# A hybrid decoder layer: the second products' sums and low parts on GpSimd, and more pairs by quarters

## The chip, the cores and the metric

The kernel runs on one core of one Trainium2 chip. A core has five engines that work at the same time and are ordered only by semaphores: TensorE (PE, matmuls and transposes; a weight load, PEld, overlaps the matmul), VectorE (DVE), ScalarE (ACT), GpSimd (POOL), and SyncE (SP), which issues the loads. Each engine takes its own instructions strictly in order. SBUF is the working memory, 128 partitions wide; PSUM holds the matmuls' results. The metric is the device time of one execution in microseconds (us).

## The reference, cut to what matters

One decoder layer on 512 tokens of width 1024, in float32: a gated feed-forward block (SwiGLU, inner width 2816), a mixer of two recurrences, and a second feed-forward block, each inside two RMS norms with a residual.

```python
def swiglu_ffn(x, w_in, w_out):
    gate, up = jnp.split(x @ w_in, 2, axis=-1)
    return (jax.nn.silu(gate) * up) @ w_out

x = x + 0.5 * rms_norm(swiglu_ffn(rms_norm(x, norm_pre[l, 0]), ffn1_w_in[l], ffn1_w_out[l]), norm_post[l, 0])
mixed = token_mixer(rms_norm(x, norm_pre[l, 1]), w_mix_in[l], conv_w[l], ...)
x = x + rms_norm(mixed, norm_post[l, 1])
x = x + 0.5 * rms_norm(swiglu_ffn(rms_norm(x, norm_pre[l, 2]), ffn2_w_in[l], ffn2_w_out[l]), norm_post[l, 2])
```

The change concerns the second product of both feed-forward blocks, the gated values (512 x 2816) times `w_out` (2816 x 1024).

## The kernel before, in words

**Three matmuls for one.** Every float32 operand is split into a high part (a rounded copy, made by ScalarE) and a low part (operand minus high part, made by a subtraction on VectorE). A product is then high x high, high x low and low x high (`mm3` and its like).

**First product (`ffn_in`, `prod`, line 572).** The inner width is 11 pairs of 256 columns (`PAIRS`). Each pair is made by the seven products of a Strassen-like scheme on quarters of the operands; sums of raw weights are made on the spot (line 263; the early ones on GpSimd, the later on VectorE). `ORDER` is the order of the products, written out by hand. The gated values land in `hf`.

**Second product (`ffn_out`).** The 1024 output columns are made in two halves of 512. In each half the 11 pairs of inner rows are gone through in the order `OUT[half]`; in the second half the last four (`LAST`: pairs 1, 3, 5, 7) are done token block by token block at the end, since norms and transposes hang on them. A pair is done in one of two ways:

- plain (`plain`, line 854): 4 token blocks x 2 column groups x 2 inner blocks x 3 = 48 matmuls of 256 columns;
- by quarters (`quartered`, `product`, line 862), for the pairs listed in `QUARTERED[half]`: seven products of 6 matmuls, 42 in all. Some go straight into the sums `C`, four into shared sums `M`, which `common` and `add` (line 824) bring into `C` once per half.

**What a pair needs.** A plain pair needs the high and low part of its gated values (`h_tile`, 1024 columns in one piece) and one split of its weights. A quartered pair needs three quarters of its gated values split (`h_quarters`: a subtraction of 256 and one of 512 columns), four sums of quarters (`h_sums`, line 805, four instructions of 256 columns), the split of these sums (`s_tile`, 1024 columns), and two splits of its weights: three quarters of them (768 columns), then four sums on the raw tile (`sum_quarters`, line 280) and a split of these (1024 columns). All copies are ScalarE's (lines 247 and 773), all subtractions and sums VectorE's (lines 249, 280, 774, 805). A pair that is quartered in both halves keeps its quarters and sums (`kept`; the sums then lie in `hf` itself, `stay`), otherwise the sums pass through the one buffer `hsum`. Pairs in `AGAIN` are plain in both halves and keep their split from the first.

**What sets the order.** `more(n)` writes the preparation of pairs two to three ahead of their use, and a scheduler orders each engine's instructions in advance; the first sums of early pairs thus stand among the first product's work. Buffers bound how far ahead anything runs: three tiles `s` for the splits of sums or plain pairs (`s_place`), places in the transposed input `xq` (`PLACES`, `LATER`) or in the ring of raw weights (`once`) for quarters, and four tiles for split weights (`WBUF`), which `feed` keeps full. Loads go out on SP's queue when a planner finds their buffer free (`load_due`). VectorE's queue also holds the work on PSUM between the products (line 591).

Of the kernel before, what the change touches and what calls it, by code (L numbers as in the profile page):

```python
# [8 lines left out]
F32 = mybir.dt.float32  # L9
F32R = mybir.dt.float32r  # L10
AF = mybir.ActivationFunctionType
ALU = mybir.AluOpType
# [41 lines left out]

QUARTERED = [(2, 3, 4, 6, 7, 8), (2, 4, 6, 8)]
OUT = [list(range(PAIRS)), [9, 2, 4, 10, 6, 8, 0, 1, 3, 5, 7]]
LAST = 4
PLACES, LATER = {2: 1, 4: 2, 6: 0, 8: 3}, {0: (1, 0), 7: (2, 3)}  # L60

AGAIN, ROWS = (9, 10), (18, 19, 20, 21)

# [24 lines left out]
class Layer:  # L90
# [678 lines left out]
            out.append(t[:, o : min(o + D, 2 * D)])  # L769
        return out  # L770

    def two_parts(self, hi, lo, src):
        self.nc.scalar.copy(hi, src)  # L773
        self.nc.vector.tensor_tensor(lo, src, hi.bitcast(F32), op=ALU.subtract)

    def h_tile(self, k2, dst=None):

        hi, lo = dst or self.s_place()
        src = self.hf[:, 2 * k2 : 2 * k2 + 2, :]
        self.two_parts(hi, lo, src)  # L780
        return hi, lo

    def h_quarters(self, k2, n=None):
# [14 lines left out]
    def h_sums(self, k2, stay):  # L798

        a = self.by_chunk(k2)  # L800
        f = self.hf[:, 2 * k2 : 2 * k2 + 2, :]
        if not stay:
            f = self.sp.tile([P, 2, T], F32, tag="xn", bufs=1, name=self.nm("hsum"))
        v = f.rearrange("p k (c u t) -> p k u c t", u=2, t=P)
        tt = lambda out, x, y, op: self.nc.vector.tensor_tensor(out, x, y, op=op)
        tt(v[:, 0, 0], a[:, 0, 1], a[:, 0, 0], ALU.subtract)
        tt(v[:, 1, 0], v[:, 0, 0], a[:, 1, 0], ALU.add)
        for k in range(2):
            tt(v[:, k, 1], a[:, k, 1], v[:, 1, 0], ALU.subtract)
        return f  # L810
# [8 lines left out]
    def ffn_out(self, gpost_row, scale, after, trans, head):  # L819
# [3 lines left out]
        nc, mm = self.nc, self.nc.tensor.matmul  # L823
        tt = lambda out, a, b, op: nc.vector.tensor_tensor(out, a, b, op=op)
        seq = [(half, k2) for half in range(2) for k2 in OUT[half]]
        made = deque((h, None) for h in self.hs)
# [3 lines left out]
        def more(n):  # L830
            while count[0] < min(n, len(seq)):
                half, k2 = seq[count[0]]
                count[0] += 1
                if k2 in QUARTERED[half]:
                    if k2 not in kept:
                        stay = k2 in QUARTERED[1]
                        kept[k2] = self.h_quarters(k2, PLACES.get(k2)), self.h_sums(k2, stay)
                    a, f = kept[k2]
                    made.append((a, self.s_tile(f)))
                elif half and k2 in AGAIN:  # L840
                    made.append(again.popleft())
                else:
                    made.append((self.h_tile(k2, self.x_place(*LATER[k2]) if half and k2 in LATER else None), None))
                    if not half and k2 in AGAIN:
                        again.append(made[-1])

# [56 lines left out]
        for half in range(2):  # L903
            C = [[self.ps() for _ in range(2)] for _ in range(2)]
            M, T, left = None, None, len(QUARTERED[half])
            for m, k2 in enumerate(OUT[half][: PAIRS - LAST * half]):
                more(n + 2)
                h, sums = made.popleft()
                if sums:
                    begin = M is None  # L910
                    if begin:
                        M = {p: self.ps() for p in ("p1", "p5", "p7", "p6")}
                    quartered(C, M, h, sums, begin)
                    left -= 1
                    if left == 0:
                        T = common(M, [self.hf[:, j, :] for j in ROWS] if half else [self.st("c") for _ in range(4)])
                else:
                    w = self.pull()
                    more(len(seq) if half and m == PAIRS - LAST - 1 else n + 3)
                    for i in (0, 2, 1, 3):  # L920
                        for v in range(2):
                            plain(C, w, h, i, v, m == 0)
                        if i > 1 and T and m == PAIRS - 1:
                            add(C, T, i % 2)
                    self.drop(w)
                n += 1
                if n == 1:
                    self.prod("p4", PAIRS - 1)
                    self.after("p4", PAIRS - 1)
                self.lag()  # L930
# [4 lines left out]
        for k2 in OUT[1][-LAST:]:  # L935
            ws.append(self.pull())
            more(n + 1)
            n += 1
# [95 lines left out]
    def ffn_items(self, name, w_in, w_out):  # L1034
# [31 lines left out]
        for h in range(2):  # L1066
            for k2 in OUT[h]:
                src = w_out[k2 * 2 * P : (k2 + 1) * 2 * P, h * 512 : (h + 1) * 512].rearrange("(k p) d -> p k d", p=P)
                key = (name, "out", h, k2)
                made.append(Item(key, [Load(key, src, 2, 512, "raw2", 5, 8)], sums=k2 in QUARTERED[h]))  # L1070
                if k2 in QUARTERED[h]:
                    made.append(Item(key, ()))
# [682 lines left out]
```

## Time and profile before

| | |
|---|---|
| median of 3 runs | 941.69 us (941.43 to 942.03) |
| profiled execution: device time, span | 942.79 us, 941.0 us |
| TensorE busy, granted clock (mean) | 932.7 us (99%), 0.998 |
| VectorE, ScalarE, GpSimd busy | 765.2, 507.7, 116.8 us |
| second products, plain and quartered pairs | from 225.4 to 342 us, and from 819.0 to 935 us |

How to read the rows: a group has its line, engine and operation, then output <- inputs by the program's names with their size, the count, the busy time in us and the mean ns of one, and last the idle time before them with what ended it. `ps` is PSUM, every other name SBUF. A timeline row has start, duration, engine, line, operation and count; a bracket gives the idle time before it and its releaser. A row of waits tells who waited for whom: total us, times, longest. A row of windows has the stretch, its length, the busy time (and count) of TensorE, its weight loads, VectorE, ScalarE and GpSimd, then the granted clock of TensorE, the share of the DMA engines and GB/s. In the slices a digit is the busy share of a fortieth of the span in tenths.

### The profile page before, as it was taken

The page shows a single profiled execution, that of the slowest core. Times are in us where ns is not written, and L with a number is a line of the kernel's source. Part 1 is how long each engine was busy: PE and PEld are TensorE (multiplying, and loading weights), DVE is VectorE, ACT ScalarE, POOL GpSimd, SP SyncE. Part 2 cuts the span into 40 slices and gives each one's busy share as a digit, 9 for nine tenths or more (in the row PEclk, how much of TensorE's full clock was granted, in tenths as well). Part 3 has the DMA queues.
Part 4 walks back from the last instruction along what each step waited for, and adds up shares of the span by engine and source line. Part 5 has one row for each costly group of instructions (what it writes and reads, how often), then busy time and mean ns, then how long its engine had stood idle before and what let it go on. Part 6 is the DMA issues. An engine that isn't in the chain of part 4 may idle for free.

```text
span 941.0 us, 18079 instructions
## 1 busy us (share of the span) xinstructions
PE 932.7 (99%) x7495; PEld 898.7 (96%) x7495; DVE 765.2 (81%) x1036; ACT 507.7 (54%) x729; POOL 116.8 (12%) x176
## 2 busy tenths in 40 slices
PE   9999999999999999999999999999999999999997
PEld 7999999999999999998887888899999999999997
DVE  6799988889988876698846665698998888998884
ACT  7645555557456467956632444565455455755541
POOL 2530000000001045200001310354000000000101
PEclk9999999999999999999999999999999999999999
DMA  9243343332352024321312124323433432224212
GB/s 314 90 156 92 121 127 113 92 111 73 116 172 90 24 86 125 107 68 46 90 45 68 46 88 135 105 77 110 138 96 108 128 120 90 91 86 127 82 46 90
DMA packets 81676, 96.12 MB, mean 102 GB/s; under 512 B 4117, under 2 KB 61497, under 8 KB 81594
## 3 DMA queue, kind: packets, MB, share of 16 engines
q1 hardware_dynamic: 81306, 94.44, 32.7%
q8 instruction: 59, 0.97, 0.4%
q10 hardware_dynamic: 288, 0.52, 0.2%
q14 instruction: 23, 0.19, 0.1%
HBM read 92.85 MB, written 2.10 MB: 101 GB/s over the span
## 4 chain that ended last, share of the span: by engine, by line
PE 62%; ACT 0%; DVE 0%; issue 0%; POOL 0%; DVEq 0%; POOLq 0%; ACTq 0%
PE ps L572 23%; PE ps L854 7%; PE ps L504 6%; PE ps L862 5%; PE ps L153 5%; PE ps L155 5%; PE ps L154 5%; PE ps L1245 2%; PE ps L321 1%; PE ps L514 1%; PE ps L1419 0%; PE ps L1330 0%; PE ps L1499 0%; PE ps L1526 0%; PE ps L1285 0%; PE ps L1523 0%
## 5 line engine op out<-in xcount | busy, mean ns | idle before, releaser
L247 ACT CAST w<-raw 128x1024 fp32r<-128x1024 f32 (+1 forms) x234 | 240.4, 1033 | 234.6 <-PE ps L572 84.4
L249 DVE TENSOR_TENSOR w<-raw,w 128x1024 fp32r<-128x1024 f32 (+1 forms) x234 | 289.4, 1243 | 41.7 <-ACT w L247 41.1
L572 PE MATMUL ps<-xq,w 128*128 128x256 f32 x2016 | 237.7, 277 | 0.2 <-ACT hf L599 0.2
L572 PEld LDWEIGHTS ps<-xq,w 128*128 128x128 f32 x2016 | 233.4, 188 | 0.4 <-ACT hf L599 0.4
L572 PE MATMUL ps<-sq,w 128*128 128x256 f32 x1440 | 169.7, 276 | 0.0
L572 PEld LDWEIGHTS ps<-sq,w 128*128 128x128 f32 x1440 | 166.5, 188 | 0.0
L854 PE MATMUL ps<-w,hs 128*128 128x256 f32 x960 | 113.0, 276 | 0.0
L854 PEld LDWEIGHTS ps<-w,hs 128*128 128x128 f32 x960 | 110.7, 188 | 0.0
L263 DVE TENSOR_TENSOR raw<-raw,raw 128x1024 f32<-128x1024 f32 x64 | 78.3, 1224 | 1.9
L153 PE MATMUL ps<-w,xq 128*128 128x512 f32 x192 | 78.9, 411 | 0.1
L155 PE MATMUL ps<-w,xq 128*128 128x512 f32 x192 | 74.9, 392 | 0.0
L154 PE MATMUL ps<-w,xq 128*128 128x512 f32 x192 | 74.8, 391 | 0.0
L409 POOL TENSOR_SCALAR col<-col 128x1 f32<-128x1 f32 x24 | 7.9, 328 | 516.4 <-ACT junk L408 516.3
L862 PE MATMUL ps<-w,hs 128*128 128x256 f32 x480 | 57.7, 276 | 0.0
L504 PE MATMUL ps<-xq,w 128*128 128x256 f32 x480 | 56.4, 278 | 0.0
L862 PEld LDWEIGHTS ps<-w,hs 128*128 128x128 f32 x480 | 55.9, 188 | 0.0
L504 PEld LDWEIGHTS ps<-xq,w 128*128 128x128 f32 x480 | 55.2, 188 | 0.5 <-issue 0.5
L263 POOL TENSOR_TENSOR raw<-raw,raw 128x1024 f32<-128x1024 f32 x16 | 42.1, 2639 | 29.5 <-DVE w L249 28.0
L153 PEld LDWEIGHTS ps<-w,xq 128*128 128x128 f32 x192 | 36.1, 188 | 8.2 <-issue 0.9
L155 PEld LDWEIGHTS ps<-w,xq 128*128 128x128 f32 x192 | 36.0, 188 | 8.2 <-DVE xq L328 0.3
L773 ACT CAST hs<-hf 128x1024 fp32r<-128x1024 f32 x32 | 33.6, 1051 | 17.7 <-PE ps L862 10.8
L154 PEld LDWEIGHTS ps<-w,xq 128*128 128x128 f32 x192 | 36.2, 188 | 6.7 <-issue 0.2
(257 smaller groups left out, 1177.7 us busy)
## 6 DMA issues: line engine op xcount, KB each, us to landing
raw<-in_ffn_w_in_dram SPq DMA_DIRECT2D x88, 512.0 KB, 4.0
raw<-in_ffn_w_out_dram SPq DMA_DIRECT2D x44, 512.0 KB, 3.8
raw<-in_w_mix_in_dram SPq DMA_DIRECT2D x28, 512.0 KB, 3.7
raw<-in_w_mix_out_dram SPq DMA_DIRECT2D x8, 512.0 KB, 3.9
out_dram<-xs SPq DMA_DIRECT2D x8, 256.0 KB, 2.0
xs<-in_x_dram SPq DMA_DIRECT2D x6, 256.0 KB, 4.4
gpost<-in_norm_post_dram SPq DMA_DIRECT2D x3, 512.0 KB, 3.5
gpre<-in_norm_pre_dram SPq DMA_DIRECT2D x2, 512.0 KB, 4.3
```

What stands on the lines that cost most here:

```text
L153: mm(ps, sh, mh, start=start, stop=False, **kw)
L154: mm(ps, sh, ml, start=False, stop=False, **kw)
L155: mm(ps, sl, mh, start=False, stop=stop, **kw)
L247: nc.scalar.copy(hi, raw)
L249: self.low = nc.vector.tensor_tensor(lo, raw, hi.bitcast(F32), op=ALU.subtract)
L263: (nc.vector if late else nc.gpsimd).tensor_tensor(o, o, c, op=ALU.add)
L504: mm(ps[:, u0:u1], w[:, a, k, :], self.xop(k, b, u0, u1), start=k + n + m == 0, stop=k == ND - 1 and n == 2, skip_group_check=True,)
L572: self.nc.tensor.matmul(ps[:, c], wb[b][:, k, v], left[d][:, k, :], start=first and a + n + k == 0, stop=n == 2 and k == KH - 1, skip_grou ...
L773: self.nc.scalar.copy(hi, src)
L854: mm(out, a[kk][:, i * P : (i + 1) * P], w[:, b, kk, QUARTER * v : QUARTER * (v + 1)], start=begin and c == kk == n == 0, stop=kk == 1 and ...
L862: mm(ps[:, QUARTER * c : QUARTER * (c + 1)], A[a][:, c], B[b], start=begin and c == n == 0, stop=n == 2, skip_group_check=True,)
L1245: nc.tensor.matmul(sc[:, 64 * m : 64 * m + 64], k8[:, m], q8[:, m], start=True, stop=True)
```

## The change

- The four sums in `h_sums` are made by GpSimd instead of VectorE.
- `two_parts` makes the low part on GpSimd unless told otherwise; `h_quarters` and `s_tile` use that. `h_tile` stays on VectorE in the first half and goes to GpSimd in the second.
- `QUARTERED` grows: in the first half pairs 2 to 9 are quartered (5 and 9 are new), in the second 2, 4, 0, 6 and 8 (0 is new). Pair 9 leaves `AGAIN`, so its plain split is made anew for the second half. Pairs 5 and 9, and 0 in the second half, have no place in `PLACES`; their quarters go to the ring of raw weights.

ScalarE's copies, the split of all weights and the sums of raw weights (lines 247, 249, 280) stay where they are. The change adds two lines: what is line 773, 774, 805, 824, 854 and 862 before is 774, 775, 806, 825, 856 and 864 after; lines up to 572 keep their numbers.

```diff
-QUARTERED = [(2, 3, 4, 6, 7, 8), (2, 4, 6, 8)]
+QUARTERED = [(2, 3, 4, 5, 6, 7, 8, 9), (2, 4, 0, 6, 8)]
 OUT = [list(range(PAIRS)), [9, 2, 4, 10, 6, 8, 0, 1, 3, 5, 7]]
...
-AGAIN, ROWS = (9, 10), (18, 19, 20, 21)
+AGAIN, ROWS = (10,), (18, 19, 20, 21)
...
-    def two_parts(self, hi, lo, src):
+    def two_parts(self, hi, lo, src, engine=None):
+
         self.nc.scalar.copy(hi, src)
-        self.nc.vector.tensor_tensor(lo, src, hi.bitcast(F32), op=ALU.subtract)
-
-    def h_tile(self, k2, dst=None):
+        (engine or self.nc.gpsimd).tensor_tensor(lo, src, hi.bitcast(F32), op=ALU.subtract)
+
+    def h_tile(self, k2, dst=None, engine=None):
 
         hi, lo = dst or self.s_place()
         src = self.hf[:, 2 * k2 : 2 * k2 + 2, :]
-        self.two_parts(hi, lo, src)
+        self.two_parts(hi, lo, src, engine or self.nc.vector)
         return hi, lo
...
-        tt = lambda out, x, y, op: self.nc.vector.tensor_tensor(out, x, y, op=op)
+        tt = lambda out, x, y, op: self.nc.gpsimd.tensor_tensor(out, x, y, op=op)
         tt(v[:, 0, 0], a[:, 0, 1], a[:, 0, 0], ALU.subtract)
         tt(v[:, 1, 0], v[:, 0, 0], a[:, 1, 0], ALU.add)
         for k in range(2):
...
-                    made.append((self.h_tile(k2, self.x_place(*LATER[k2]) if half and k2 in LATER else None), None))
+                    dst = self.x_place(*LATER[k2]) if half and k2 in LATER else None
+                    made.append((self.h_tile(k2, dst, nc.gpsimd if half else None), None))
```

## The prediction

> **What bounds the kernel now.** First the page: busy shares and the slices of the span.
>
> ```profile
> PE 932.7 (99%) x7495; PEld 898.7 (96%) x7495; DVE 765.2 (81%) x1036; ACT 507.7 (54%) x729; POOL 116.8 (12%) x176
> PE   9999999999999999999999999999999999999997
> DVE  6799988889988876698846665698998888998884
> POOL 2530000000001045200001310354000000000101
> ```
>
> TensorE has no hole but at the very end, VectorE is second, GpSimd almost empty. The waits of TensorE, asked next, are two, together 1.7 us:
>
> ```profile
> PE ps L149 <- POOL ident masks.py:199: 1.5, 1, 1.5
> PE ps L572 <- ACT hf L599: 0.2, 1, 0.2
> ```
>
> So the time is the number of matmuls times their rate, as long as every operand is ready. The timeline of TensorE in the second products (both feed-forward blocks) gives the rate and the deadlines; the first row below is VectorE's, the start of the preparation (first quarters of the gated values):
>
> ```profile
> 210.62 1.02 DVE L774 TENSOR_TENSOR xq<-hf,xq 128x256 fp32r<-128x256 f32 x2
> 225.44 5.60 PE L854 MATMUL ps<-w,hs 128*128 128x256 f32 x48
> 230.88 2.88 PE L572 MATMUL ps<-xq,w 128*128 128x256 f32 x24
> 239.03 1.52 PE L862 MATMUL ps<-w,xq 128*128 128x256 f32 x12
> 240.40 2.88 PE L862 MATMUL ps<-w,hs 128*128 128x256 f32 x24
> 243.12 0.84 PE L862 MATMUL ps<-w,xq 128*128 128x256 f32 x6
> 243.79 1.52 PE L862 MATMUL ps<-w,once 128*128 128x256 f32 x12
> 273.04 16.48 PE L854 MATMUL ps<-w,hs 128*128 128x256 f32 x144
> 832.63 1.52 PE L862 MATMUL ps<-w,xq 128*128 128x256 f32 x12
> 866.63 16.48 PE L854 MATMUL ps<-w,hs 128*128 128x256 f32 x144
> ```
>
> A plain pair takes 48 matmuls, 230.88 - 225.44 = 5.44 us; a pair by quarters 42, 243.79 - 239.03 = 4.76 us. Pair 2 starts at 239.03, and pair 9 of the first half, still plain, runs from 273.04 to 278.48. The second block has the same distance: 866.63 - 832.63 = 34.00, as 273.04 - 239.03. I work out one block and double it.
>
> **The change, part 1: matmuls.** Pairs 5 and 9 in the first half and 0 in the second become quartered, in both blocks: 6 x (5.44 - 4.76) = -4.1 us if nothing waits.
>
> **Part 2: what VectorE gets and loses.** Prices, from the groups by form, GpSimd's line 263, and the timelines:
>
> ```profile
> L263 POOL TENSOR_TENSOR raw<-raw,raw x16: 2392/2410/3437, 23.9 to 648.4; 128x1024 f32<-128x1024 f32 x16
> L774 DVE TENSOR_TENSOR hs<-hf,hs 128x1024 fp32r<-128x1024 f32 x32 | 39.0, 1219 | 1.3 <-ACT hs L773 1.2
> L805 DVE TENSOR_TENSOR hf<-hf 128x256 f32<-128x256 f32 x32 | 13.3, 421 | 0.6
> 247.25 2.42 DVE L249 TENSOR_TENSOR w<-raw,w 128x1024 fp32r<-128x1024 f32 x2
> 250.72 0.95 DVE L249 TENSOR_TENSOR w<-raw,w 128x768 fp32r<-128x768 f32 x1
> 257.50 1.81 DVE L280 TENSOR_TENSOR raw<-raw 128x256 f32<-128x256 f32 x4
> 259.40 1.05 ACT L247 CAST w<-raw 128x1024 fp32r<-128x1024 f32 x1 [3.32 <-DVE raw L280]
> 283.45 0.19 POOL L409 TENSOR_SCALAR col<-col 128x1 f32<-128x1 f32 x1 [225.49 <-ACT junk L408]
> ```
>
> The weights of a quartered pair cost VectorE a low part of 768 columns, four sums and a low part of 1024: 0.95 + 1.81 + 1.21 = 3.97 us, where a plain one costs 1.21. What leaves VectorE per freshly quartered pair is four sums (4 x 0.42), two quarter subtractions (256 and 512 columns, 1.02 together by the 210.62 row) and one of 1024 (1.22), some 3.9 us.
>
> **Part 3: the same work on GpSimd.** The trace has only the 1024-column form there: 2.41 us alone. An instruction on one column takes 0.19, so a straight line through both gives 0.77 for 256 columns and 1.31 for 512 (estimates). In the built order GpSimd does eight sums during the first products, well ahead. From the first quarters on it has, until pair 9 can start, 33 instructions of 256 columns, 8 of 512 and 8 of 1024 (eight pairs' quarters and low parts, 25 sums). Alone that is 25.4 + 10.5 + 19.3 = 55.2 us: started at 210.62 it ends at 265.8, ahead of pair 9 at 239.03 + 7 x 4.76 = 272.4. Were this all, nothing would wait.
>
> **Part 4: the two engines exclude each other.** Timeline rows of the places where GpSimd already runs such an addition:
>
> ```profile
> 23.93 4.89 POOL L263 TENSOR_TENSOR raw<-raw,raw 128x1024 f32<-128x1024 f32 x2 [2.66 <-DVE w L249]
> 25.99 0.69 DVE L354 TENSOR_TENSOR xq<-ps,xq 128x512 fp32r<-128x512 f32 x1 [0.94 <-ACT xq L355]
> 27.91 1.99 DVE L249 TENSOR_TENSOR w<-raw,w 128x1024 fp32r<-128x1024 f32 x1 [0.25 <-ACT w L247]
> 41.51 2.39 POOL L263 TENSOR_TENSOR raw<-raw,raw 128x1024 f32<-128x1024 f32 x1 [6.65 <-DVE w L249]
> 42.40 2.59 DVE L249 TENSOR_TENSOR w<-raw,w 128x1024 fp32r<-128x1024 f32 x1 [0.36 <-ACT w L247]
> 52.13 1.22 DVE L249 TENSOR_TENSOR w<-raw,w 128x1024 fp32r<-128x1024 f32 x1
> 52.17 5.80 POOL L263 TENSOR_TENSOR raw<-raw,raw 128x1024 f32<-128x1024 f32 x2 [1.17 <-DVE col L1092]
> 53.27 2.35 DVE L1093 TENSOR_TENSOR col<-prm,col 128x4 f32<-128x4 f32 x1
> 56.22 2.83 DVE L249 TENSOR_TENSOR w<-raw,w 128x1024 fp32r<-128x1024 f32 x1
> 636.69 2.35 DVE L249 TENSOR_TENSOR w<-raw,w 128x1024 fp32r<-128x1024 f32 x2
> 637.98 5.67 POOL L263 TENSOR_TENSOR raw<-raw,raw 128x1024 f32<-128x1024 f32 x2 [7.03 <-DVE w L249]
> ```
>
> GpSimd runs from 41.51 to 43.90; a weight subtraction put out at 42.40 ends at 44.99, 1.09 after it, so it stood still meanwhile. The same at 27.91 (ends 1.08 after 28.82) and 56.22 (1.08 after 57.97). Even four columns at 53.27 took 2.35 us. It holds the other way: at 637.98 the pair ends at 643.65, 4.61 after VectorE's 639.04, so the first of the two took 4.61 - 2.41 = 2.20 from there. A subtraction that reads PSUM (25.99, 0.69 us) isn't held. So a GpSimd addition and a VectorE instruction with both inputs in SBUF take turns, instruction by instruction, and their times add. The Trainium skill says the same ("SBUF — State Buffer", section "Who interferes with whom"): a VectorE instruction with two SBUF inputs and a GpSimd one that reads SBUF contend, and the second blocks until the first is done. The trace agrees (2.59 against 1.21 us); by that rule the change loses, and without it the time would be part 1's.
>
> Everything VectorE does for weights (lines 249, 280) is of that kind, so the sum of both queues is what counts. A GpSimd instruction that waited for its turn has its start-up behind it: 2.22 for 1024 columns (2.41 - 0.19), and by the same cut 1.12 and 0.58. I take these, since 49 of them meet about as many of VectorE's; the prices alone (55.2) are the upper end. GpSimd: 33 x 0.58 + 8 x 1.12 + 8 x 2.22 = 45.9 us. VectorE in the same stretch: six of 1024 columns (the last first-product weights, pairs 0, 1 and 10) 7.3, and eight pairs' weights 8 x 3.97 = 31.8, together 39.0. So the last weights of pair 9 are ready at 210.62 + 45.9 + 39.0 = 295.5; the 24 matmuls on them take 2.72 (240.40 to 243.12), and pair 9 ends at 298.2 instead of 278.5: +19.7. With the prices alone it is +29.0. The faster matmuls of pairs 5 and 9 are lost in this wait.
>
> To that come stretches in which neither can go. Between a pair's sums and its last low part ScalarE copies the weights (1.05, the 259.40 row) and VectorE waits; GpSimd fills this except where its own next instruction waits for a later ScalarE copy, by the built order at pairs 7, 8 and 9: 3 x 1.05 = 3.2. Bounds: 0, and all eight, 8.4.
>
> **Part 5: the second half.** Per quartered pair both queues need 2.22 + 3.97 = 6.2 against 4.76: 7.2 us too much over five, and pair 0's quarters and sums 3.4 more. The plain pairs 10, 9 and again 10 give back 2 x 4.2 + 2.0 = 10.4. Nothing left, so 0; bounds -1 and +5. Pair 0 saves 0.68. The low part of pair 5, the third of the last four, can start when pair 0's sums leave their buffer (0.68 before pair 0 ends) and is wanted 2.72 after: 3.4 us for 1.05 + 2.41 and a VectorE turn of 1.21, so +1.3. Pair 9 is no longer kept, which is one 1024 more, counted above. Pairs 5, 9 and 0 put their quarters into the ring of raw weights, so two loads for the mixer, and what stands behind them on SP's queue, go out at pair 0's end; four plain pairs (4 x 5.44 = 21.8 us) hide them; without these a landing of some 4 us would show.
>
> **Sum.** Per block 19.7 + 3.2 + 0 - 0.7 + 1.3 = 23.5 us, twice 47.0. The profiled execution took 942.79 us (span 941.0) and gives 989.8; the median of 941.69 gives **989 us**, 5% slower.
>
> **Rivals.** (a) The turns don't bind here and GpSimd alone matters: its queue is done at 265.8, pair 9 wants it at 272.4, TensorE never waits, 941.69 - 4.1 = **937.6 us**, faster. For it: 6.6 us of slack, and VectorE is relieved of 6 x 3.9 + 9 x 1.22 - 3 x 2.76 = 26 us per block (nine 1024-column low parts of the second half leave it too; three pairs' weights are added). Against: every GpSimd addition that met a weight subtraction held it. It decides from the point where both queues together fit between 210.62 and 272.4 (61.7 us); I count 84.9.
>
> (b) The stalls also lower TensorE's clock. The windows at the end of the span show that it falls:
>
> ```profile
> 935.00:938.00 3.00, 0.00 (x0) 0.00 (x0) 1.84 (x3) 0.45 (x2) 0.81 (x2) 0.99 0.00 0
> 938.00:941.00 3.00, 0.00 (x0) 0.00 (x0) 0.00 (x0) 0.00 (x0) 0.00 (x0) 0.50 0.47 175
> ```
>
> The third number from the right is the granted clock: 0.99, then 0.50, once TensorE has had no matmul for about 3 us (its last here end at 934.8). The Trainium skill states it as a rule ("TensorE: Matmul & The Clock Gate", section "What's actually happening"): after an idle window of about 3.4 us the clock is halved until one such window has been busy; the trace agrees at this one place. My sum leaves 298.2 - 239.0 - 8 x 4.76 = 21 us of holes in eight pairs, under 3 us each, so I take the full clock. At half clock a pair takes 9.52 and the eight end at 239.0 + 76.2 = 315.2, 17 us later; if that holds for half of the stretch, twice 8.5 is added: **1006 us**.
>
> (c) The change could fail to do what it says, if the built program kept the sums on VectorE or the pairs plain. It doesn't: the built order shows them on GpSimd and 42 matmuls for each new pair. No chance is set aside.
>
> **How the numbers follow.** The taking of turns has every meeting in the trace behind it, so the forecast of 989 us gets 0.73; its own range is 981 (no idle stretches, -1 in the second half: 2 x 4.2 less) to 1028 (per block +9.3 for the prices alone, +5.2 for all idle stretches, +5 in the second half). Rival (a) has 0.10, since the short forms and saturated queues appear nowhere; rival (b) 0.15; a stall that just eats the 4 us 0.02. The range of 968 to 1030 leaves out (a); it takes in (b) and 13 us below the forecast's own low end, as the 84.9 us of both queues rest on two estimated forms (33 x 0.58 + 8 x 1.12 = 28.1; a quarter less is 7 per block). Faster by over 0.2% 0.10, within 0.2% (2 us, about what runs of this kernel, 941.43 to 942.03, can tell from no change) 0.02, slower 0.88.
>
> **What would show it.** Part 1: 36 matmuls fewer. Part 3: GpSimd's busy time up by some 2 x 80 us or more, since waiting counts as busy there. Part 4: VectorE's line 249 mean well above 1243 ns, GpSimd's 256-column form far above 0.77 where both are busy; TensorE idle behind line 249's low parts or line 775's in pairs 3 to 9 of the first half, in both blocks; pair 9 ending about 20 us later. Part 5: few holes in the second half. Rival (a) shows a TensorE without holes; (b) a granted clock below 1.00 in the first half. I would be wrong if turns go by something other than whole instructions, if the short forms cost much more than the line through two points, or if the in-order queues lock each other out for longer than I counted.

## The result and the profile after

The changed kernel takes 1016.57 us (median of 4 runs, 1015.07 to 1018.4) beside 941.86 us for the kernel before on the same chip: 1.0791 times the time before, 95% interval 1.0769 to 1.0813. Its profiled execution has a span of 1015.0 us, 74.0 more than before, and a mean granted clock of 0.979 instead of 0.998.

The page of the changed kernel, busy shares, the slices of TensorE and of its clock:

```profile
PE 956.2 (94%) x7459; PEld 913.6 (90%) x7459; DVE 818.4 (81%) x960; ACT 516.3 (51%) x749; POOL 342.3 (34%) x320
PE   9999999998688799999999999999999999778877
PEclk9999999999899899999999999999999999989989
```

There are 36 matmuls fewer, as forecast, and still TensorE is busy for 23.5 us longer. The holes lie in two stretches, the second products of the two blocks. The waits of TensorE in the changed kernel (for whom, us in total, times, longest):

```profile
PE ps L864 <- ACT w L247: 29.6, 16, 4.9
PE ps L864 <- DVE w L249: 14.4, 18, 0.9
PE ps L864 <- DVE y L446: 3.9, 2, 2.0
PE ps L864 <- POOL hs L775: 1.9, 2, 0.9
PE ps L149 <- POOL ident masks.py:199: 1.5, 1, 1.5
PE ps L856 <- POOL hs L775: 0.8, 2, 0.5
```

That is 52.1 us of waits where the kernel before had 1.7. The additional 50.4 us of waits and 23.5 us of busy time make up the 74.0 us. Of the waits 44.0 us are for weights (lines 247 and 249), 3.9 for the norm between the halves (`y`) and only 2.7 for a low part that GpSimd makes. So TensorE hardly waits for GpSimd itself; it waits for the engines that make the weights. VectorE's and GpSimd's groups by form show the cause:

```profile
L249 DVE TENSOR_TENSOR w<-raw,w 128x1024 fp32r<-128x1024 f32 x214 | 290.2, 1361 | 62.8 <-ACT w L247 62.0
L280 DVE TENSOR_TENSOR raw<-raw 128x256 f32<-128x256 f32 x104 | 103.9, 999 | 3.2
L249 DVE TENSOR_TENSOR w<-raw,w 128x768 fp32r<-128x768 f32 x26 | 43.7, 1681 | 3.3 <-ACT w L247 3.3
L775 POOL TENSOR_TENSOR hs<-hf,hs 128x1024 fp32r<-128x1024 f32 x26 | 70.0, 2697 | 62.6 <-ACT hs L774 62.6
```

A sum of raw weights (line 280) takes 999 ns on the mean, 0.42 us in the kernel before; the low part of 768 columns 1681 ns, 0.95 before; a low part of 1024 columns on GpSimd takes 2.70 us, where 2.41 is what one takes alone. Both engines stand still in turn, and standing still counts as busy.

Where the time goes within a block is read from TensorE's timeline. First half of the columns, first block:

```profile
237.85 1.52 PE L864 MATMUL ps<-w,xq 128*128 128x256 f32 x12
...
256.12 0.58 PE L864 MATMUL ps<-w,hs 128*128 128x256 f32 x1 [3.19 <-ACT w L247]
257.44 3.99 PE L864 MATMUL ps<-w,hs 128*128 128x256 f32 x17 [0.73 <-DVE w L249]
...
266.93 2.27 PE L864 MATMUL ps<-w,hs 128*128 128x256 f32 x17 [0.88 <-DVE w L249]
...
274.10 0.38 PE L864 MATMUL ps<-w,hs 128*128 128x256 f32 x1 [2.08 <-ACT w L247]
275.36 3.42 PE L864 MATMUL ps<-w,hs 128*128 128x256 f32 x17 [0.88 <-DVE w L249]
...
296.47 1.60 PE L864 MATMUL ps<-w,once 128*128 128x256 f32 x12
...
301.30 11.04 PE L856 MATMUL ps<-w,hs 128*128 128x256 f32 x96
```

Pair 2 starts at 237.85 and pair 9 ends at 301.30: 63.45 us, where the kernel before needed 278.48 - 239.03 = 39.45. The first half lost 24.0 us. The rows at 256.12 and 257.44 also show the clock: after a hole of 3.19 us, seventeen matmuls take 3.99 us, which take 2.27 us at 266.93. A shorter hole, 2.08 us with one matmul and 0.88 us more behind it, was enough to slow part of the next seventeen (3.42 us at 275.36). Pair 9 itself, from 296.47 on, runs through without a wait; the time is lost in the pairs before it. Second half of the columns:

```profile
314.28 1.64 PE L864 MATMUL ps<-w,xq 128*128 128x256 f32 x12 [1.94 <-DVE y L446]
...
348.84 0.58 PE L864 MATMUL ps<-w,hs 128*128 128x256 f32 x1 [4.82 <-ACT w L247]
350.10 4.00 PE L864 MATMUL ps<-w,hs 128*128 128x256 f32 x17 [0.68 <-DVE w L249]
...
354.93 3.11 PE L856 MATMUL ps<-w,hs 128*128 128x256 f32 x26
...
379.55 5.66 PE L514 MATMUL ps<-xq,w 128*128 128x256 f32 x44
```

Line 514, the work behind the second products, starts at 379.55; before it started at 343.17. From the end of pair 9 that is 78.25 us against 64.69: the second half lost another 13.6 us. Pair 0 alone, from 341.42 to 354.93, takes 13.5 us, of which 4.82 are one wait and then the half clock. What VectorE, ScalarE and GpSimd do around that wait:

```profile
338.40 5.56 POOL L775 TENSOR_TENSOR hs<-hf,hs 128x1024 fp32r<-128x1024 f32 x2 [4.85 <-ACT hs L774]
341.74 5.90 DVE L280 TENSOR_TENSOR raw<-raw 128x256 f32<-128x256 f32 x4
343.91 2.52 POOL L775 TENSOR_TENSOR xq<-hf,xq 128x1024 fp32r<-128x1024 f32 x1
347.75 1.99 ACT L247 CAST w<-raw 128x1024 fp32r<-128x1024 f32 x2 [7.74 <-DVE raw L280]
```

The four sums of pair 0's weights (1.81 us when nothing holds them) come out at 341.74, while GpSimd is in the second of three low parts of 1024 columns. They end at 347.64, after the third (346.43). ScalarE has waited 7.74 us for them, TensorE 4.82. The windows of the changed kernel give the clock by stage (columns as in the profile before):

```profile
238.00:301.00 63.00, 47.35 (x335) 44.67 (x334) 54.00 (x46) 25.39 (x33) 45.28 (x31) 0.89 0.23 69
301.00:355.00 54.00, 44.80 (x360) 43.32 (x359) 46.86 (x51) 24.50 (x39) 28.90 (x21) 0.94 0.25 77
885.00:940.00 55.00, 42.74 (x302) 40.87 (x303) 47.90 (x45) 22.29 (x28) 36.91 (x26) 0.88 0.25 77
```

### The profile page after: what moved, and what is told of

Same layout as the page of the kernel before. It is cut to its first block, busy times and chain, and to the rows that moved or that the text cites. A ratio compares the mean times of both kernels' runs of the same rounds, so it can differ in the third digit from the quotient of the medians.

```text
span 1015.0 us, 18156 instructions
## 1 busy us (share of the span) xinstructions
PE 956.2 (94%) x7459; PEld 913.6 (90%) x7459; DVE 818.4 (81%) x960; ACT 516.3 (51%) x749; POOL 342.3 (34%) x320
## 5 line engine op out<-in xcount | busy, mean ns | idle before, releaser
L247 ACT CAST w<-raw 128x1024 fp32r<-128x1024 f32 (+1 forms) x240 | 244.3, 1027 | 305.9 <-DVE raw L280 128.8
L249 DVE TENSOR_TENSOR w<-raw,w 128x1024 fp32r<-128x1024 f32 (+1 forms) x240 | 333.0, 1395 | 66.1 <-ACT w L247 65.2
L864 PE MATMUL ps<-w,hs 128*128 128x256 f32 x624 | 96.7, 308 | 45.9 <-ACT w L247 29.6
L864 PEld LDWEIGHTS ps<-w,hs 128*128 128x128 f32 x624 | 86.1, 211 | 53.4 <-ACT w L247 32.8
L806 POOL TENSOR_TENSOR hf<-hf 128x256 f32<-128x256 f32 x40 | 43.6, 1099 | 227.4 <-DVE hf L591 226.1
L280 DVE TENSOR_TENSOR raw<-raw 128x256 f32<-128x256 f32 x104 | 103.9, 999 | 3.2
L856 PE MATMUL ps<-w,hs 128*128 128x256 f32 x768 | 91.6, 277 | 0.8 <-POOL hs L775 0.8
L775 POOL TENSOR_TENSOR hs<-hf,hs 128x1024 fp32r<-128x1024 f32 x26 | 70.0, 2697 | 62.6 <-ACT hs L774 62.6
L856 PEld LDWEIGHTS ps<-w,hs 128*128 128x128 f32 x768 | 89.1, 188 | 1.2 <-POOL hs L775 1.2
L864 PE MATMUL ps<-w,xq 128*128 128x256 f32 x288 | 41.1, 294 | 3.9 <-DVE y L446 3.9
L153 PEld LDWEIGHTS ps<-w,xq 128*128 128x128 f32 x192 | 36.1, 188 | 8.2 <-issue 0.9
```

Source lines behind the costliest of these rows:

```text
L153: mm(ps, sh, mh, start=start, stop=False, **kw)
L247: nc.scalar.copy(hi, raw)
L249: self.low = nc.vector.tensor_tensor(lo, raw, hi.bitcast(F32), op=ALU.subtract)
L280: self.nc.vector.tensor_tensor(b[out], b[a], b[c], op=ALU.add)
L775: (engine or self.nc.gpsimd).tensor_tensor(lo, src, hi.bitcast(F32), op=ALU.subtract)
L856: mm(out, a[kk][:, i * P : (i + 1) * P], w[:, b, kk, QUARTER * v : QUARTER * (v + 1)], start=begin and c == kk == n == 0, stop=kk == 1 and ...
```

## The experiments

The theory on test is Part 4's: GpSimd's additions and VectorE's two-input instructions exclude each other, and that makes the weights late. Its rivals: that the additional quartered pairs alone cost the time, that it is waits of GpSimd's own chain, and, later, whether the sum of both engines' times or the order of their work sets the loss.

**The engines alone, the pairs alone.** The first kernel keeps the new engines with the old pairs, the second the new pairs with all work on VectorE.

```diff
# engines alone (against the changed kernel)
-QUARTERED = [(2, 3, 4, 5, 6, 7, 8, 9), (2, 4, 0, 6, 8)]
+QUARTERED = [(2, 3, 4, 6, 7, 8), (2, 4, 6, 8)]
-AGAIN, ROWS = (10,), (18, 19, 20, 21)
+AGAIN, ROWS = (9, 10), (18, 19, 20, 21)
# pairs alone: the same two lines the other way, against the kernel before
```

> The change of engines without the new quartered pairs (six in the first half, four in the second, as before). Turns (VectorE and GpSimd exclude each other where both read SBUF): a quartered pair takes about 8.4 us in the first half instead of 4.76, as in the changed kernel, six of them, less the slack of the plain pair 5: about 15 us per block there and 5 in the second half, so 982 us (965 to 1000). Rival, GpSimd is simply too slow for eight pairs: with six its queue ends earlier still, 942 us. Rival, the weights of the added pairs are the cost: 942 us.

Measured: 970.04 us, ratio 1.0297 (1.0280 to 1.0314), so 28 us slower: within the range, 12 under the figure.

> The new quartered pairs without the change of engines: all sums and low parts on VectorE. Turns: GpSimd is idle, so only VectorE's own queue counts; up to pair 9 it holds 39.0 us for weights and 28.5 for the moved work, 67.5 from 210.6, so pair 9 ends near 281 instead of 278.5: 2 to 6 us more per block, 946 us (938 to 956). Rival, the added pairs are the cost of the change: about 1016 us.

Measured: 949.53 us, ratio 1.0076 (1.0061 to 1.0091), 7.5 us slower. This is within the range. The pairs save 36 matmuls (4.1 us) and lose more than that: behind the start-up TensorE waits 4.6 us, 3.7 of them for the weights of quartered pairs, and part of the remainder is a slower rate of the matmuls, told at the end of this section. The two parts cost 28 and 7.5 us alone and 74.7 together, so they are not independent. My reading is that the new pairs give VectorE more sums and low parts of weights exactly where GpSimd's additions hold it.

**Additional work on GpSimd, nothing else changed.** Two pairs of kernels add work to GpSimd in the kernel before, at the places where the change gives it work; VectorE keeps all of its own. In the first pair GpSimd reads the tiles of the second products:

```diff
+    def extra(self, x, like):       # after each low part and sum of VectorE's
+        ...
# extra reads
+        self.nc.gpsimd.tensor_tensor(o, x, x, op=ALU.subtract)
# extra writes: one column read, then two fills
+        self.nc.gpsimd.tensor_copy(one(o), one(x))
+        for _ in range(2):
+            self.nc.gpsimd.memset(o, 0.0)
```

> The kernel before, all work where it was, and beside it about the same additions once more on GpSimd (both inputs from the same SBUF tiles, result into a scratch tile that nobody reads; 1024 columns as two of 448, 512 as 448). Nothing in the products waits for a GpSimd result. Turns: VectorE is held anyway, and it still has its own 7.9 us per quartered pair, so slower than the change of engines alone, 1010 us (985 to 1045), and the mean of the weight subtractions (line 249) goes up by 10% or more. Rival, the change loses because TensorE waits for GpSimd's results: 942 us.

Measured: 1006.67 us, ratio 1.0688 (1.0661 to 1.0716), with VectorE's sums of raw weights at 711 ns instead of 422. The time is as forecast; the mean of the weight subtractions (line 249) rose by 4% (1298 ns instead of 1243), not by 10% or more.

> The same extra work on GpSimd, but as memsets of the scratch tile: each a copy of one column, for the place in time, and two memsets of 256 or 448 columns, so GpSimd is busy about as long and reads next to nothing. Turns only where GpSimd reads SBUF (so the Trainium skill, SBUF - State Buffer, Who interferes with whom): 942 us (940 to 948). Rival, any GpSimd instruction holds VectorE: near the time with extra reads, 985 us or more.

Measured: 982.92 us, ratio 1.0437 (1.0414 to 1.0461): a miss by 41 us. VectorE was not held (its sums take 421 ns, its weights 1269). What the forecast overlooked: the one-column copies read the tiles of the ring, so that a buffer comes free only when GpSimd's queue has passed it. ScalarE's timeline in the run with fills:

```profile
260.87 1.04 ACT L774 CAST hs<-hsum 128x1024 fp32r<-128x1024 f32 x1 [8.40 <-POOL scratch L792]
```

TensorE's largest wait there, 14.2 us in two, is another one: for `y` of line 446, which comes up again with the next two kernels. The run with reads has no such wait of ScalarE for GpSimd; ScalarE waits there for VectorE's sums of raw weights, 103.7 us in all against 33.5 in the kernel before. So the two runs lose their time in different ways and can't be set against each other. The second pair of kernels starts GpSimd's work from a tile of its own that ScalarE fills (at the places of the sums from one column of the gated values). The additions read `xs`, the tile of the residual stream, which the second products leave alone until their post norm; it is not the table of constants that the forecast below names. Up to the end of pair 9 no engine waits for a result of this work.

```diff
# both; 204 additions, at the low parts and sums of the kernel before
+            mark = self.hp.tile([P, 1], F32, tag="mark", bufs=16, name=self.nm("mark"))
+            self.nc.scalar.copy(mark, hi[...])
+        self.nc.gpsimd.tensor_copy(o[:, :1], mark)
# reads
+        self.nc.gpsimd.tensor_tensor(o, self.xs[:, 0, :n], self.xs[:, 1, :n], op=ALU.subtract)
# fills
+        for _ in range(2):
+            self.nc.gpsimd.memset(o, 0.0)
```

> The kernel before, unchanged in what VectorE and TensorE do; beside it GpSimd makes 204 additional subtractions of two operands, 128x192 each, into a scratch tile, at the places where the changed kernel gives it low parts and sums; they read a table of constants and not the tiles of the second products, so that no buffer of the ring waits for GpSimd's queue (ScalarE copies one column into a small tile of its own, and GpSimd starts from that). If an addition with two operands keeps VectorE out while it runs: some 150 us of additions, about half of them in the bound stretches: 980 us (962 to 1000), with the mean of the 128x1024 weights over 1290 ns against 1270. If the loss of the changed kernel came only from longer waits of its own chains: 942 to 947 us, and unchanged VectorE means.

> The same with the addition replaced by two fills (no operand read) of the same scratch tile: the same queue and the same starts, but nothing that reads with two operands. If only GpSimd's work with two operands keeps VectorE out: 943 us (940 to 950). If any use of GpSimd at these places costs, or the one-column copies do: about as much as the run with additions.

Measured: 1023.33 us with reads (1.0853, 1.0837 to 1.0869), 978.48 us with fills (1.0376, 1.0357 to 1.0395). Both lie above what I wrote, the fills by 35 us. TensorE's waits, of the run with fills and then of the run with reads, name the reason:

```profile
PE ps L882 <- DVE y L446: 25.7, 2, 12.8
```
```profile
PE ps L881 <- DVE y L446: 37.7, 4, 18.0
PE ps L881 <- ACT w L247: 5.2, 2, 2.7
PE ps L881 <- DVE w L249: 4.1, 6, 1.2
```

`y` of line 446 belongs to the post norm between the halves, and its column steps (line 409) run on GpSimd too. In the run with fills they stood behind the additional work until 302.45, and ScalarE waited 16.9 us for them. That part is the price of GpSimd's queue, which I forgot for this place. The first half of the columns lies ahead of it and is free of it. With fills TensorE starts pair 2 at 237.62 and the plain pairs at 271.62, 34.00 us apart as in the kernel before; with reads 280.86 - 238.74 = 42.12 us. VectorE's groups, of the run with fills and then of the run with reads:

```profile
L280 DVE TENSOR_TENSOR raw<-raw 128x256 f32<-128x256 f32 x80 | 33.7, 421 | 1.6
L249 DVE TENSOR_TENSOR w<-raw,w 128x768 fp32r<-128x768 f32 x20 | 19.0, 949 | 0.0
```
```profile
L280 DVE TENSOR_TENSOR raw<-raw 128x256 f32<-128x256 f32 x80 | 47.5, 594 | 1.7
L249 DVE TENSOR_TENSOR w<-raw,w 128x768 fp32r<-128x768 f32 x20 | 22.4, 1118 | 0.0
```

So GpSimd instructions with two operands in SBUF, on data that the second products don't touch there, hold VectorE and cost 8.1 us per block in that stretch; fills of the same tile at the same places hold nothing and cost it nothing. The Trainium skill ("SBUF — State Buffer", section "Who interferes with whom") says that a GpSimd instruction that only writes doesn't contend with a VectorE instruction of two SBUF inputs; the means of 421 and 949 ns agree.

**The second half given back to VectorE.**

```diff
# against the changed kernel
-                    made.append((a, self.s_tile(f)))
+                    made.append((a, self.s_tile(f, nc.vector if half else None)))
...
-                    made.append((self.h_tile(k2, dst, nc.gpsimd if half else None), None))
+                    made.append((self.h_tile(k2, dst, nc.vector if half else None), None))
```

> The changed kernel with the low parts of the second half of the columns given back to VectorE (pair 0's sums stay with GpSimd, the first half is as in the changed kernel). My account after the result: the second half lost 13.6 us per block because VectorE's chains stood behind GpSimd's 128x1024 low parts one after another; without them most of it comes back: 995 us (985 to 1003), pair 0's wait for ScalarE's weights under 1 us instead of 4.8. If the second half's loss is only what the first half's delay leaves behind, or pair 0's quarters themselves: 1010 to 1017 us.

Measured: 996.72 us, ratio 1.0572 (1.0555 to 1.0589). The wait of pair 0 is gone, and 19.9 us of the 27 us that the second halves had lost come back. Pair 0's quarters stay with GpSimd in this kernel, like its sums. The first half is as slow as in the changed kernel: from pair 2 at 238.43 to the end of pair 9 at 302.90, 64.47 us.

**Which of the two kinds of work.** One kernel gives VectorE back the sums, one the low parts.

```diff
# sums back
-        tt = lambda out, x, y, op: self.nc.gpsimd.tensor_tensor(out, x, y, op=op)
+        tt = lambda out, x, y, op: self.nc.vector.tensor_tensor(out, x, y, op=op)
# low parts back
-        (engine or self.nc.gpsimd).tensor_tensor(lo, src, hi.bitcast(F32), op=ALU.subtract)
+        (engine or self.nc.vector).tensor_tensor(lo, src, hi.bitcast(F32), op=ALU.subtract)
-                    made.append((self.h_tile(k2, dst, nc.gpsimd if half else None), None))
+                    made.append((self.h_tile(k2, dst, nc.vector if half else None), None))
```

> The changed kernel with the 80 sums of 128x256 given back to VectorE (0.42 us each there, about 0.80 on GpSimd when nothing holds it); the low parts stay with GpSimd. If the two engines take turns, the stretches that they bound get shorter by about 80 x (0.80 - 0.42) = 30 us: 986 us (968 to 1000). If GpSimd's queue for itself were the limit: 80 x 1.1 = 88 us off it, and the kernel falls to 940 to 955. If VectorE's own work were the limit: 34 us more, 1035 to 1050.

Measured: 1016.32 us, ratio 1.0785 (1.0767 to 1.0803), no gain at all. All three figures missed. The total hides two effects that cancel. Ahead of the second products one of VectorE's sums now stands behind a low part of GpSimd's (1.51 us instead of 0.42) and holds up VectorE's work on PSUM, so that TensorE waits in the first product:

```profile
215.84 2.98 PE L572 MATMUL ps<-sq,w 128*128 128x256 f32 x24 [1.37 <-DVE ps L591]
```

Pair 2 starts at 240.42 instead of 237.85. Pair 9 ends at 301.05 instead of 301.30, so the first half takes 60.63 us instead of 63.45, 2.8 less. Of a block's 40 sums only 15 lie in that stretch in the changed kernel; at Part 4's prices (0.58 on GpSimd, 0.42 on VectorE) they are worth 2.4 us. The run therefore refutes the 30 us of its own expectation, which counted all 80 at 0.80, but not Part 4's sum.

> The changed kernel with all low parts back on VectorE; only the 80 sums of 128x256 stay with GpSimd. After the run with the sums given back (no gain) my account is that the low parts alone close the loop: ScalarE makes a weight copy, then the copy of a gated pair, GpSimd starts its two 128x1024 low parts (2.6 us each) and keeps VectorE from the four sums of the next weights, for which ScalarE waits. Then this kernel lies near the kernel with the pairs alone (949.5): 955 us (947 to 966). If what counted were the sum of the two engines' times, the sums hold VectorE for 80 x 0.80 = 64 us and save it 34: 972 to 990 us.

Measured: 964.95 us, ratio 1.0237 (1.0224 to 1.0250), inside the first range near its end. Counted from the pairs alone (949.53), the sums on GpSimd cost 15.4 us, the low parts 66.8 (1016.32), both together 67.0 (1016.57). On top of the low parts the sums cost nothing in the total. The order of the work in the changed kernel suggests why; VectorE, GpSimd and ScalarE around the hole of 3.19 us:

```profile
248.18 6.73 DVE L280 TENSOR_TENSOR raw<-raw 128x256 f32<-128x256 f32 x4
249.59 2.55 POOL L775 TENSOR_TENSOR hs<-hf,hs 128x1024 fp32r<-128x1024 f32 x1
252.10 2.53 POOL L775 TENSOR_TENSOR hs<-hsum,hs 128x1024 fp32r<-128x1024 f32 x1
255.03 1.78 ACT L247 CAST w<-raw 128x1024 fp32r<-128x1024 f32 x2 [6.92 <-DVE raw L280]
256.71 1.04 ACT L774 CAST hs<-hf 128x1024 fp32r<-128x1024 f32 x1
258.82 5.66 DVE L280 TENSOR_TENSOR raw<-raw 128x256 f32<-128x256 f32 x4
```

It is a round. VectorE's four sums wait behind two long low parts (one by one they take 0.84, 0.85, 2.48 and 2.46 us); ScalarE, in order, waits for the sums (6.92 us) and only then copies the weights and after them the next gated pair; that copy lets GpSimd's next low parts go, which meet VectorE's next four sums. This round, the longest, takes 258.82 - 248.18 = 10.6 us, where a quartered pair needs 4.76 on TensorE; the eight pairs take 63.45 us, 7.9 each on the mean. This account says what should help: shorter pieces, even though they are longer in sum.

```diff
# against the changed kernel; the 34 low parts of 128x1024 on GpSimd
+            for k in range(2):
+                for c in (slice(0, T // 2), slice(T // 2, T)):
+                    self.nc.gpsimd.tensor_tensor(lo[:, k, c], src[:, k, c], hi[:, k, c], op=ALU.subtract)
```

> The changed kernel with GpSimd's 34 low parts of 128x1024 made as four pieces of 128x256 each, the numbers computed being the same. A piece of that shape takes about 0.80 us where nothing holds it, so a low part becomes longer in sum, 3.2 us against 2.2 to 2.7. If the engines only exclude each other and the sum of their times is what bounds: 34 x (0.5 to 1.0) = 17 to 34 us slower, 1033 to 1050 us. If the loss comes from VectorE's short chain (four sums, for which ScalarE waits) standing behind two long low parts, VectorE gets its turn after 0.8 us instead of 2.6: the sums of 128x256 for the weights take on the mean about 0.8 instead of 1.00 us, and the kernel is faster than the changed one: 1000 us (985 to 1012).

Measured: 1001.78 us, ratio 1.0640 (1.0622 to 1.0657), 14.8 us faster than the changed kernel (by the two medians). Groups of that kernel, VectorE's sums of weights, then GpSimd's pieces:

```profile
L280 DVE TENSOR_TENSOR raw<-raw 128x256 f32<-128x256 f32 x104 | 85.0, 817 | 3.2
L779 POOL TENSOR_TENSOR hs<-hf,hs 128x256 fp32r<-128x256 f32 x104 | 112.8, 1115 | 19.5 <-ACT hs L774 19.5
L779 POOL TENSOR_TENSOR hs<-hsum,hs 128x256 fp32r<-128x256 f32 x32 | 32.0, 1028 | 0.0
```

GpSimd is busy with these low parts for 144.8 us instead of 92.3, and the kernel is faster. TensorE now waits 31.3 us for GpSimd's own output (its waits for `once`, 12.9, and for `hs`, 12.3 and 6.1) and 5.4 for weights. So the shorter pieces let the weights through and make GpSimd late itself.

**A version that might beat both.** If GpSimd is the trouble, single new pairs may pay with everything on VectorE.

```diff
-QUARTERED = [(2, 3, 4, 6, 7, 8), (2, 4, 6, 8)]
+QUARTERED = [(2, 3, 4, 6, 7, 8), (2, 4, 0, 6, 8)]     # pair 0
+QUARTERED = [(2, 3, 4, 5, 6, 7, 8), (2, 4, 6, 8)]     # pair 5
```

> The kernel before with one edit of the change: pair 0 by quarters in the second half of the columns, everything on VectorE. Twelve matmuls less, 2 x 6 x 0.1133 us = 1.4 us, if VectorE's longer weights (3.97 against 1.21 us) and sums find room there, as in the second half of the kernel with the pairs alone, where TensorE waits for nothing: 940.7 us (939.5 to 942). If VectorE is the limit in the second half too: 943 to 946.

> The kernel before with pair 5 by quarters in the first half, everything on VectorE, pair 9 kept for the second half as before. Twelve matmuls less (1.4 us) against VectorE's additional work in the first half, which in the kernel with the pairs alone showed TensorE waiting 3.3 us for weights with pairs 5 and 9: 941 us (939.8 to 944). If one more pair is already too much for VectorE: 943 to 946 us.

Measured: 945.07 us for pair 0 (1.0025, 1.0016 to 1.0034) and 946.89 for pair 5 (1.0047, 1.0034 to 1.0059). The forecasts were 940.7 and 941; the first lies in the range given for a VectorE that is the limit, the second 0.9 above it. Both save 12 matmuls and are slower. TensorE's waits, pair 0 and then pair 5:

```profile
PE ps L514 <- ACT w L247: 1.4, 1, 1.4
PE ps L854 <- DVE hs L774: 1.1, 2, 0.5
PE ps L854 <- DVE w L249: 0.4, 2, 0.2
```
```profile
PE ps L862 <- DVE w L249: 3.2, 4, 1.2
```

With pair 0 the low part of pair 5 comes late in the last four pairs, and the mixer's first weights wait 1.4 us in the first block. That its quarters sit in the ring and hold back a load is my reading of this; it was not tried apart. With pair 5 VectorE is the limit in the first half. To be 2.4 and 4.2 us slower (by the medians) with 1.4 us of matmuls fewer they must lose 3.8 and 5.6; TensorE's waits behind the start-up are 3.2 and 3.7. With pair 5 the trace shows where more of it goes. Behind a wait of 1.18 us the matmuls follow one another at 0.118 us instead of 0.113 for long stretches, at a granted clock of 1.00: the second half of the columns, the same work as in the kernel before and without a wait, takes 48.05 us (291.34 to 339.39) instead of 46.24 (289.36 to 335.60). What sets this slower rate no run shows. None of the kernels run beats the one before.

## Why the prediction came out as it did

The forecast was 989 us, its own range 981 to 1028, the full range 968 to 1030; the time is 1016.57. Direction, place and mechanism hold; the size is 28 us short, and one term, the second half of the columns, carries nearly all of that.

- **Part 1** holds: 7459 matmuls instead of 7495. As forecast, the saving is lost in waits.
- **Part 2** holds as a price and not as a duration: with the pairs alone VectorE's sums and low parts of 768 columns take 417 and 950 ns, with GpSimd's additions beside them 999 and 1681.
- **Part 3** holds for the short form (a sum of 256 columns that meets nothing takes 0.79 us at 254.71; the estimate was 0.77). GpSimd's busy time rose by 225.5 us, "some 2 x 80 us or more". The conclusion "were this all, nothing would wait" was rival (a), and the runs with additional reads refute it.
- **Part 4, the turns,** is shown: additions with two operands hold VectorE, fills don't. **Its size** came out right: the first half lost 24.0 us per block, the steps gave 19.7 + 3.2, and part 1's saving was counted in. **Its arithmetic** did not hold. "The sum of both queues is what counts" fails where GpSimd's low parts are cut: they are busy for 144.8 us instead of 92.3, and the first half takes 58.73 us (238.34 to 297.07) instead of 63.45. The run with the sums given back doesn't decide it (2.8 us less there, 2.4 by Part 4's prices). And the chain of the sum was another: it ended with the last weights of pair 9, but pair 9 runs without a wait, and the time is lost in pairs 3 to 8. What the runs fit is the round: the longest instruction that VectorE's four sums can stand behind, with ScalarE's order closing the loop. The agreement to 1.1 us is therefore in part luck. The prediction names this only in its last clause ("if the in-order queues lock each other out for longer than I counted").
- **Part 5, the second half,** is the term that failed: predicted 0 with bounds of -1 and +5, together with pair 0's -0.68 and the last four's +1.3 some 0.6 us per block; measured 13.6, so 26 us more over two blocks, nearly the whole difference. I compared two totals (both queues against TensorE's time) and found nothing left over. The stretch is not short of time on the whole; it is short where three of GpSimd's low parts follow one another on VectorE's four sums. Of the 13.6 us, TensorE's waits are 9.7 (pair 0's alone 5.50), and most of the rest the half clock behind them. With the second half's low parts given back to VectorE, the kernel takes 19.9 us less. The last four take 0.7 us longer (354.93 to 379.55 against 319.27 to 343.17), forecast as 1.3; the ring's loads, costed at nothing, show no wait in the changed kernel, and the 1.4 us in the kernel with pair 0 alone may be theirs.
- **Rival (b), the clock,** was put beside the forecast and belonged into it. I took holes "under 3 us each" and the full clock. There were holes of 3.19 and 4.82 us, and the stages show 0.89 and 0.94. TensorE's busy time is 23.5 us longer with 4.1 us of matmuls fewer, 27.6 us more than they need at the full rate. At most some 19 us of that are the clock (a mean of 0.979 over 1015.0 us loses 21.3 us, one of 0.998 over 941.0 loses 1.9); most of the other part lies in the matmuls right in front of some 40 holes, whose ends no next matmul covers (0.38 us for the single one at 274.10, 0.113 in an unbroken run). That isn't all loss, as I read it: in the first half TensorE waits for weights anyway, and a slower pair only shortens the next wait, so the first half could come out as forecast with this left out. In the second half it adds to pair 0's wait. No run takes the clock apart from the waits. The Trainium skill's rule ("TensorE: Matmul & The Clock Gate", section "What's actually happening": halved after an idle window of about 3.4 us) agrees only roughly: the hole of 3.19 us was enough, and in part already the one of 2.08 us with a single matmul and 0.88 us more behind it.
- **Rival (c)** did not occur.

## What to carry to other kernels

Where two engines exclude each other, an instruction moved from one to the other costs its length at the moment when something short and urgent stands behind it. Totals of the two engines said little here; look for the shortest chain that feeds the bound engine, and for the longest instruction that it can meet. Long exclusive instructions cut into pieces can be faster although they are longer in sum. And where the bound engine is TensorE, holes of 2 to 3 us can cost twice, since matmuls behind them ran at half the clock here.

## What the hardware showed that I had not expected

- Fills on GpSimd don't hold VectorE at all: 408 fills of 128x192 beside it leave the sums of weights at 421 ns and the first half at 34.00 us.
- Effects add badly: 28 us and 7.5 us alone are 74.7 together, and 15.4 and 66.8 are 67.0.
- VectorE in turn holds even a GpSimd copy of a single column: in the run with fills such copies mostly take from 0.18 us up to 1.23, beside fills of 0.26 on the mean. I read it as the same turns, since the copy reads SBUF and the fill doesn't. One copy per block takes 6.86 us, until VectorE has gone through twelve two-input instructions without a break; its row and that of the last of the twelve:

```profile
223.18 6.86 POOL L788 COPY scratch<-mark 128x1 f32<-128x1 f32 x1
228.78 1.21 DVE L776 TENSOR_TENSOR hs<-hf,hs 128x1024 fp32r<-128x1024 f32 x1
```

The copy ends at 230.04, VectorE's row at 229.99. So the turns don't always go instruction by instruction, as Part 4 has it; what decides who goes next no run shows.
